# A decoder layer on one core: two small block transfers cut in four, and one PSUM bank of the first phase given to other work

## The chip, the cores and the metric

The kernel runs on one core of a Trainium2 chip. The metric is the device time of one execution in microseconds (us); less is better. Three runs of the kernel before gave 2307.01 to 2318.52 us, with a median of 2308.78 us.

## The reference

One layer of a hybrid decoder is computed for a prompt of 4096 tokens (model width 1024) and for 8 single-token samples. The input is scaled and shifted, projected once, and split into two head groups. Group A is a gated delta rule in chunks, group B an attention with a window of 128. Both are gated, projected back and normalised. The change lies in group A of the prompt:

```python
lower = eye + beta[..., :, None] * jnp.einsum('nbhtd,nbhid->nbhti', k, k) * dec_strict
rhs = jnp.concatenate([(beta * jnp.exp(G))[..., None] * k, beta[..., None] * v], -1)
sol = lax.linalg.triangular_solve(lower, rhs, left_side=True, lower=True, unit_diagonal=True)
...
def step(s, xs):
    w_c, ut_c, aqk_c, qd_c, kd_c, gl_c = xs
    u = ut_c - jnp.einsum('bhcd,bhde->bhce', w_c, s)
    o = jnp.einsum('bhcd,bhde->bhce', qd_c, s) + jnp.einsum('bhti,bhie->bhte', aqk_c, u)
    s = gl_c[..., None, None] * s + jnp.einsum('bhcd,bhce->bhde', kd_c, u)
    return s, o
```

## The kernel before, in words

The work has three phases. The first, which the change touches, makes group A of the prompt in 16 steps of 256 tokens; beside it run the preparation of later weights and the samples' part of group A. The second makes group B in 32 tiles of 128 tokens, and the third the gates, the output projection and the normalisation.

A step of phase one treats two chunks of 128 tokens and four heads, so eight 128 by 128 triangular systems. `front` projects the keys, queries and values (PSUM tile `pj`, lines 300 to 322, with the short convolution on VectorE, L315), takes the decays (tile `pga`, L348), transposes the keys, queries and values (tile `tr`, L355, L389, L399), and multiplies keys by keys and queries (tile `pga`, read by L379 into `U` and by L382 into `Aqk`, four tiles in a step).

`lanes` inverts the 32 by 32 diagonal blocks of the eight systems. It stores them from `U` to a scratch array in HBM in four DMAs (L411), loads them back as `LU`, each block repeated in four groups of 32 partitions (L413), and runs a loop of 31 pairs of VectorE instructions (L420 and L422). The loop works on `LV`, which is first reset from a constant (L415). It stores the result (L424) and loads it back in another order in four DMAs (L429) as `VTd`. Then `gdn_inv` doubles the block size twice (L432 to L480, for each chunk a chain that goes from TensorE to ScalarE, to VectorE and back several times), and `gdn_c` steps the state (L491 to L519).

Side work takes small PSUM tiles from `xt_ps`: the gate's columns (L174, 8 tiles), the samples (`dec_a`, 27 tiles; two for each sample, read by L666 and L678), and the second half of the weights' preparation (`prep_s`, 8 tiles, read by L550). That is 43 tiles in the phase.

PSUM has eight banks here: one for `pga`, one for `xt`, one for `tr`, two for `pj`, three for `pgi` (`gdn_inv` and `gdn_c`). A tile that takes a bank again waits until the last reader of the bank's former tile is done.

The order of the instructions on each engine is set when the program is built. A scheduler goes through all of them with its own estimates of durations, pools and buffers, so that the steps overlap: the loop of one step runs while the next step's projections are made. Each engine then takes its list in that order, and an instruction that waits holds up what is behind it in its own list. All DMAs of the phase's steps are issued by SyncE (SP), in its list's order.

Of the kernel before, what the change touches and what calls it, by code (L numbers as in the profile page):

```python
# [14 lines left out]
PSUM = bass.MemoryType.PSUM  # L15
# [18 lines left out]
def body(ctx, tc, I, O, seq):  # L34
# [3 lines left out]
    pe, act, dve, pool, sp = nc.tensor, nc.scalar, nc.vector, nc.gpsimd, nc.sync  # L38
# [72 lines left out]
    with ExitStack() as p1:  # L111
# [4 lines left out]
        stg = p1.enter_context(tc.tile_pool(name="stg", bufs=2))  # L116
        wk = p1.enter_context(tc.tile_pool(name="wk", bufs=2))
        sml = p1.enter_context(tc.tile_pool(name="sml", bufs=2))
        pga = p1.enter_context(tc.tile_pool(name="pga", bufs=1, space=PSUM))
        pxt = p1.enter_context(tc.tile_pool(name="pxt", bufs=1, space=PSUM))  # L120
        pst = p1.enter_context(tc.tile_pool(name="pst", bufs=1, space=PSUM))
        pj = p1.enter_context(tc.tile_pool(name="pj", bufs=2, space=PSUM))
        pgi = p1.enter_context(tc.tile_pool(name="pgi", bufs=3, space=PSUM))
# [2 lines left out]
            return pst.tile(shape, dt, name="tr")  # L126

        def xt_ps(shape, dt=F32):
            return pxt.tile(shape, dt, name="xt")

        def load_x(s):

# [31 lines left out]
        def gate_cols():  # L164
            part, dst, one = 2, gateT, 1.0
            for blk in range(8):
                cc = part * 8 + blk
                ps = xt_ps([128, 9])
                for hf in range(2):
                    st = stg.tile([128, 4, 256], F32, name="stg")[:, 0:2].rearrange("p a (b c) -> p (a b) c", c=128)  # L170
                    sp.dma_start(st, I["wg"][blk][:, 4 * hf:4 * hf + 4])
                    for k in range(4):
                        mm(ps, st[:, k, :], cT[:, 4 * hf + k, :], hf + k == 0, hf + k == 4)
                dve.tensor_scalar(dst[:, blk, :], ps, cols[:, cc:cc + 1], one, op0=ALU.add, op1=ALU.add)  # L174
                yield
# [84 lines left out]
        def front(s, hT, ahead):  # L260
# [109 lines left out]
            for c in range(2):  # L370
                cs = slice(c * 128, (c + 1) * 128)
                for hp in range(2):
# [8 lines left out]
                    m = 4 * c + 2 * hp  # L381
                    dve.tensor_mul(Aqk[:, m:m + 2, :], pa[:, :, 0, :], decs[c][:, 2 * hp:2 * hp + 2, :])  # L382
            vt, vt16 = lanes(s, U)
            act.activation(U16[:, 0], U, AF.Copy)
            dve.tensor_sub(U16[:, 1], U, U16[:, 0])
# [19 lines left out]
        def lanes(s, U):  # L405

            d1, d2 = D1[s % 2], D2[s % 2]
            d1v = d1.rearrange("(m b) (i t) -> b i m t", b=4, t=32)
            for b in range(4):
                bs = slice(32 * b, 32 * b + 32)  # L410
                sp.dma_start(d1v[b], U[bs, :, bs])  # L411
            LU = w1p.tile([128, 32, 32], F32, name="LU", bufs=1)
            sp.dma_start(LU.rearrange("p a b -> p (a b)"), d1[None].to_broadcast([4, 32, 1024]))  # L413
            LV = w1p.tile([128, 8, 32], F32, name="LV", bufs=1)
            dve.tensor_copy(LV.rearrange("p a b -> p (a b)"), lv0)  # L415
            lt = w1p.tile([128, 8, 32], F32, name="lt", bufs=1)
            for j in range(31, 0, -1):
                j0 = j // 4
                n = 8 - j0
                dve.tensor_mul(lt[:, j0:, 0:j], LV[:, j0:, j:j + 1].to_broadcast([128, n, j]),  # L420
                               LU[:, None, 0:j, j].to_broadcast([128, n, j]))
                dve.tensor_add(LV[:, j0:, 0:j], LV[:, j0:, 0:j], lt[:, j0:, 0:j])  # L422
            d2w = d2.rearrange("l (j c i) -> c l j i", c=4, i=32)
            sp.dma_start(d2w, LV)  # L424
            d2r = d2.rearrange("(m b) (q i) -> b q m i", b=4, i=32)
            vt = VTd
            for b in range(4):
                bs = slice(32 * b, 32 * b + 32)
                sp.dma_start(vt[bs, :, bs], d2r[b])  # L429
            vt16 = w1p.tile([128, 2, 8, 2, 32], F16, name="vt16")  # L430
            ve = vt.rearrange("p m (a b) -> p m a b", b=64)[:, :, :, 0:32]
            act.activation(vt16[:, 0], ve, AF.Copy)  # L432
            dve.tensor_sub(vt16[:, 1], ve, vt16[:, 0])
            return vt, vt16
# [98 lines left out]
        def prep_s(i):  # L533
# [7 lines left out]
            if blk == 0:  # L541
                act.activation(b, b, AF.Copy, scale=WS)
            else:
                gp = xt_ps([128, 2, 2, 128])
                for h in range(2):
                    mm(gp[:, h], gateT[:, 4 * h + u, 0:1].to_broadcast([128, 128]),
                       ident[:, None, :].to_broadcast([128, 2, 128]))
                for row in range(2):
                    q = b[:, 2 * row:2 * row + 2].rearrange("p a b -> p (a b)")
                    dve.scalar_tensor_tensor(q, q, WS, gp.rearrange("p a b c -> p (a b c)"),  # L550
                                             op0=ALU.mult, op1=ALU.mult)
                act.activation(b[:, 0:2], b[:, 0:2], AF.Copy, scale=normc)
# [21 lines left out]
        def dec_a():  # L574
            dt_ = wf
            us_ps = xt_ps([128, 12, 16])
            for blk in range(12):
                w = w1[blk]
# [159 lines left out]
    with ExitStack() as p2:  # L738
# [14 lines left out]
        pst = p2.enter_context(tc.tile_pool(name="pst2", bufs=2, side="right", space=PSUM, **W2))  # L753
# [701 lines left out]
```

## Time and profile before

| what | value |
|---|---|
| median of three runs | 2308.78 us |
| the profiled execution, its own time | 2309.84 us |
| its span, first to last instruction | 2308.1 us |
| TensorE matmul busy | 2119.3 us, 92% |
| VectorE busy | 1834.1 us, 79% |
| ScalarE busy | 1266.6 us, 55% |
| GpSimd busy | 162.0 us, 7% |
| granted TensorE clock, mean | 0.969 |
| share of the last-ending chain: TensorE, VectorE, DMA, ScalarE | 42%, 17%, 7%, 6% |

Busy times overlap between engines. A busy matmul row is not a matmul at its peak, since matmuls are pipelined and their ends are modelled. The chain is followed back from the last instruction: at each step to what released it, or to the instruction ahead of it on its engine. Line numbers are those of the kernel before.

### The profile page before, as it was taken

What the parts mean: (1) busy time and instruction counts of PE and PEld (TensorE: products, weight loads), DVE (VectorE), ACT (ScalarE), POOL (GpSimd) and SP (SyncE); (2) the same over time, 40 slices, a digit from 0 to 9 for tenths busy, and PEclk for the clock granted to TensorE, in tenths of its full rate; (3) what the DMA queues carried; (4) which work ended last, traced back from release to release, by engine and by line L of the source; (5) the groups of instructions that cost most, each with busy time, mean ns of one, the idle gap of its engine ahead of it and who ended that gap; (6) DMA issues with size and microseconds to landing.
All of it is one profiled execution on the core that took longest, in us unless ns stands there. A gap on an engine that the chain in (4) does not pass through costs nothing.

```text
span 2308.1 us, 48753 instructions
## 1 busy us (share of the span) xinstructions
PE 2119.3 (92%) x18287; PEld 1516.0 (66%) x18287; DVE 1834.1 (79%) x5546; ACT 1266.6 (55%) x3601; POOL 162.0 (7%) x284
## 2 busy tenths in 40 slices
PE   6988798898989898899899999999999999999997
PEld 4867677787877787787576777777545454444443
DVE  7778677888888788888767977777687788898877
ACT  6755656666666576666455666666632333434332
POOL 1111110111111011110000000000000000000000
PEclk9999999999999999999899999999999999999999
DMA  8332322323333123222334311111342343333322
GB/s 321 117 114 67 88 88 72 101 89 94 124 101 98 60 76 99 77 67 79 97 102 165 113 59 63 58 59 39 125 169 74 115 141 105 115 106 111 108 91 74
DMA packets 139757, 232.18 MB, mean 101 GB/s; under 512 B 60933, under 2 KB 73529, under 8 KB 133353
## 3 DMA queue, kind: packets, MB, share of 16 engines
q1 hardware_dynamic: 138224, 228.52, 29.5%
q8 instruction: 144, 2.36, 0.4%
q14 instruction: 93, 0.75, 0.1%
q10 hardware_dynamic: 1296, 0.55, 0.1%
HBM read 154.07 MB, written 76.09 MB: 100 GB/s over the span
## 4 chain that ended last, share of the span: by engine, by line
PE 42%; DVE 17%; DMA 7%; ACT 6%; issue 2%; SPq 1%; POOL 0%; POOLq 0%; ACTq 0%; DVEq 0%
PE pp L1040 21%; PE pj L41 9%; DMA LU<-D 3%; PE pgi L41 3%; DVE kqv L315 2%; ACT Sm L870 2%; PE po L41 2%; DVE lt L420 2%; PE tr L887 2%; DVE LV L422 1%; PE tr L41 1%; PE pS L41 1%; DMA D<-LV 1%; DVE bst L1075 1%; PE pga L41 1%
## 5 line engine op out<-in xcount | busy, mean ns | idle before, releaser
L41 PE MATMUL pj<-hT,w 128*128 128x256 f16 x4608 | 578.8, 276 | 3.4 <-ACT hT L255 2.6
L41 PEld LDWEIGHTS <-w 128*128 128x128 f16 x4800 | 452.8, 99 | 62.2 <-issue 6.8
L1040 PEld LDWEIGHTS <-S 128*128 128x128 f16 x1536 | 150.4, 99 | 170.7 <-issue 3.6
L41 PEld LDWEIGHTS <-hT 128*128 128x128 f16 x2048 | 159.8, 98 | 69.3 <-issue 2.0
L41 PE MATMUL pj<-wq,hT 128*128 128x512 f16 x768 | 191.8, 379 | 0.0
L315 DVE SCALAR_TENSOR_TENSOR kqv<-u,cols,kqv 128x256 f32<-128x256 f32 x384 | 181.4, 478 | 2.7 <-ACT kqv L313 2.1
L1040 PE MATMUL pp<-wz,S 128*128 128x512 f16 x768 | 181.1, 382 | 0.0
L870 ACT ACTIVATE Sm<-Sm,nm 128x256 f32<-128x256 f32 (+1 forms) x256 | 125.5, 492 | 92.4 <-DVE nm L867 92.3
L1040 PE MATMUL pp<-wo,S 128*128 128x512 f16 x768 | 171.3, 379 | 0.7 <-DVE zs L1216 0.6
L420 DVE TENSOR_TENSOR lt<-LV,LU 128x60 f32<-128x60 f32 (+24 forms) x496 | 119.4, 241 | 54.9 <-DMA LU<-D 48.8
L1040 PE MATMUL pp<-wz,hT 128*128 128x512 f16 x576 | 133.0, 382 | 1.2 <-ACT zs L1127 1.2
L863 DVE CUSTOM_DVE_ANT_0 Sm<-pS,swam 128x256 f32<-128x256 f32 (+1 forms) x256 | 96.4, 415 | 35.5 <-PE tr L887 32.0
L1040 PE MATMUL pp<-wo,A 128*128 128x512 f16 x540 | 122.1, 379 | 0.0
L41 PE MATMUL pj<-wkv,hT 128*128 128x256 f16 x768 | 107.7, 275 | 0.4 <-ACT v L814 0.4
L1040 PEld LDWEIGHTS <-hT 128*128 128x128 f16 x612 | 60.1, 99 | 72.7 <-issue 4.4
L422 DVE TENSOR_TENSOR LV<-LV,lt 128x60 f32<-128x60 f32 (+24 forms) x496 | 102.6, 207 | 6.2
L41 PE MATMUL pga<-kqv 128*128 128x256 f32 x256 | 75.3, 409 | 25.7 <-DVE kqv L322 25.7
L1079 POOL TENSOR_TENSOR rs<-rs,cf 128x1 f32<-128x1 f32 (+1 forms) x33 | 22.8, 692 | 1077.1 <-DVE rs L1078 1077.1
L1040 PEld LDWEIGHTS <-A 128*128 128x128 f16 x540 | 52.9, 99 | 62.0
L1021 ACT ACTIVATE S<-zt 128x512 f16<-128x512 f32 x64 | 40.2, 630 | 85.3 <-DVE zt L1027 81.1
L1134 ACT ACTIVATE zs<-zs 128x512 f32<-128x512 f32 x48 | 30.2, 629 | 100.5 <-DVE zs L1133 100.5
L315 DVE SCALAR_TENSOR_TENSOR vv<-u,cols,vv 128x256 f32<-128x256 f32 x192 | 82.6, 479 | 1.7 <-ACT vv L313 0.9
(378 smaller groups left out, 4607.0 us busy)
## 6 DMA issues: line engine op xcount, KB each, us to landing
hT<-hD SPq DMA_DIRECT2D x32, 1024.0 KB
x<-in_xT_dram SPq DMA_DIRECT2D x32, 512.0 KB
hD<-hT SPq DMA_DIRECT2D x16, 1024.0 KB
x<-in_x_prompt_dram SPq DMA_DIRECT2D x60, 256.0 KB
out_y_prompt_dram<-x SPq DMA_DIRECT2D x60, 256.0 KB
stg<-in_ws_dram SPq DMA_DIRECT2D x16, 512.0 KB
LU<-D SPq DMA_DIRECT2D x16, 512.0 KB
wS<-wt SPq DMA_DIRECT2D x16, 512.0 KB
```

Source lines behind the costliest of these rows:

```text
L41: pe.matmul(out, l, r, start=st, stop=sp_)
L315: dve.scalar_tensor_tensor(d, u[:, b2, j:j + 256], cwj(j, blk), d, op0=ALU.mult, op1=ALU.add)
L420: dve.tensor_mul(lt[:, j0:, 0:j], LV[:, j0:, j:j + 1].to_broadcast([128, n, j]), LU[:, None, 0:j, j].to_broadcast([128, n, j]))
L422: dve.tensor_add(LV[:, j0:, 0:j], LV[:, j0:, 0:j], lt[:, j0:, 0:j])
L863: dve.tensor_tensor_reduce(Sm[:, h, k0:256], pS[:, h2, k0:256], swam[:, k0:256], 0.125, -1e30, op0=ALU.add, op1=ALU.max, accum_out=mx[:, h ...
L870: act.activation(Sm[:, h, k0:256], Sm[:, h, k0:256], AF.Exp, bias=nm[:, h:h + 1], accum_out=sm_[:, h:h + 1])
L887: pe.transpose(pt[:, h2, kb, :], Sm[:, h + h2, kb * 128:(kb + 1) * 128], ident)
L1021: act.activation(q[:, 0], src, AF.Copy)
L1040: pe.matmul(dst.rearrange("p (u c) -> p u c", c=128), A[:, hi, k, :], W[:, k // 2::2, q, wi, k % 2, :], start=new and n == 0, stop=n == 11 ...
L1075: dve.bn_stats(st[0:n, q, :], r[q][0:n])
L1079: pool.tensor_tensor(rs[0:n, 1:2], rs[0:n, 0:1], half_neg[0:n, 0:1], op=ALU.pow)
L1134: act.activation(zs, zs, AF.Silu, scale=IWS)
```

## The change

The load of `LU` and the store of `LV` become four DMAs each, one for each group of 32 partitions. The pool `xt` goes; what took its tiles now takes them from the single bank of `tr`, and `pga` gets two banks.

```diff
-        pga = p1.enter_context(tc.tile_pool(name="pga", bufs=1, space=PSUM))
-        pxt = p1.enter_context(tc.tile_pool(name="pxt", bufs=1, space=PSUM))
+        pga = p1.enter_context(tc.tile_pool(name="pga", bufs=2, space=PSUM))
...
         def xt_ps(shape, dt=F32):
-            return pxt.tile(shape, dt, name="xt")
+            return pst.tile(shape, dt, name="tr")
...
             LU = w1p.tile([128, 32, 32], F32, name="LU", bufs=1)
-            sp.dma_start(LU.rearrange("p a b -> p (a b)"), d1[None].to_broadcast([4, 32, 1024]))
+            for c in range(4):
+                sp.dma_start(LU[32 * c:32 * c + 32].rearrange("p a b -> p (a b)"), d1)
...
             d2w = d2.rearrange("l (j c i) -> c l j i", c=4, i=32)
-            sp.dma_start(d2w, LV)
+            for c in range(4):
+                sp.dma_start(d2w[c], LV[32 * c:32 * c + 32])
```

The scheduler answers with another order over the whole of phase one. The instructions that compute are the same in kind and number; only SP has more, 6 in a step. Three places follow. In the rows of the change, lines between the two edits are one less than before, and lines behind the second are one more.

VectorE in the ninth step, the last rows ahead of the loop's first instruction, which reads `LU`. Before:

```order
L451 TENSOR_TENSOR Vo<-V,Vo 128x256
L451 TENSOR_TENSOR XE<-pgi,XE 128x8x32
L678 SCALAR_TENSOR_TENSOR stg<-xt,dkq,stg 128x128
L322 SCALAR_TENSOR_TENSOR vv<-th,vv 128x1024
L466 COPY V<-pgi 32x4x32
L467 COPY V<-pgi 32x4x32
L678 SCALAR_TENSOR_TENSOR stg<-xt,dkq,stg 128x128
L256 TENSOR_TENSOR hT<-x,hT 128x512
L451 TENSOR_TENSOR VR<-V,VR 64x256
L256 TENSOR_TENSOR hT<-x,hT 128x512
L451 TENSOR_TENSOR V_319<-pgi,V_319 64x256
L420 TENSOR_TENSOR lt<-LV,LU 128x31
```

And with the change:

```order
L321 SCALAR_TENSOR_TENSOR vv<-th,vv 128x1024
L452 TENSOR_TENSOR XZ<-pgi,XZ 64x4x64
L255 TENSOR_TENSOR hT<-x,hT 128x512 x3
L452 TENSOR_TENSOR Vo<-V,Vo 128x256
L452 TENSOR_TENSOR XE<-pgi,XE 128x8x32
L467 COPY V<-pgi 32x4x32
L468 COPY V<-pgi 32x4x32
L452 TENSOR_TENSOR VR<-V,VR 64x256
L452 TENSOR_TENSOR V_316<-pgi,V_316 64x256
L667 TENSOR_TENSOR dt_9690<-tr,deg 128x4
L420 TENSOR_TENSOR lt<-LV,LU 128x31
```

From the last instruction that fills `U` to that first read of `LU` there were 24 instructions, and there are 27. The second chunk's chain of `gdn_inv` (`Vo` to `V`) stood between other work and now stands in one piece.

VectorE again, from the loop's end of the step ahead to the reset of `LV`, with the change (`vv` and `kqv` are projections, `sc` and `sse` are small vectors):

```order
L422 TENSOR_TENSOR LV<-LV,lt 128x8
L314 SCALAR_TENSOR_TENSOR kqv<-u,cols,kqv 128x256
L321 SCALAR_TENSOR_TENSOR kqv<-th,kqv 128x1024
L359 TENSOR_SCALAR sse<-sse 128x8
...
L314 SCALAR_TENSOR_TENSOR vv<-u,cols,vv 128x256 x6
L378 SCALAR_TENSOR_TENSOR U<-pga,sc,dec 128x128 x2
L381 TENSOR_TENSOR Aqk<-pga,dec 128x256
L378 SCALAR_TENSOR_TENSOR U<-pga,sc,dec 128x128 x2
L381 TENSOR_TENSOR Aqk<-pga,dec 128x256
L415 COPY LV<-cf 128x256
```

All work on the way from the loop's end to the reset is shown but four instructions on small vectors. Behind the reset come four more on `U` and one on `Aqk` before the first that needs `VTd` (L434).

TensorE, in one step, where the weights' preparation takes its product of the gate and the next step's small projection `wbd` begins. Before, in two banks:

```order
L41 MATMUL pgi<-VR,XZ 128x64
L41 MATMUL pgi<-S,kqv 128x128 x4
L41 MATMUL pgi<-r,V 128x128 x4
L41 MATMUL xt<-cf,gateT 128x256
L41 LDWEIGHTS hT
L41 MATMUL tr<-wbd,hT 128x16
```

With the change, in one bank; 29 matmuls lie between the product of the gate and the first on `wbd`:

```order
L41 MATMUL pgi<-S,kqv 128x128 x5
L41 MATMUL tr<-cf,gateT 128x256 x2
L41 LDWEIGHTS w_7_363
L41 MATMUL pj<-hT,w_7_363 128x256
...
L41 MATMUL pgi<-ut,Kd 128x128 x4
L41 MATMUL pgi<-ut,Aqk 128x128 x4
L41 LDWEIGHTS hT
L41 MATMUL tr<-wbd,hT 128x16
```

The side products stood at any place among the transposes. Now, in this step, the three of them (two of a sample, one of the gate) stand behind the step's last transposes, each with 23 to 27 other matmuls ahead of it.

## Rows read from the trace of the kernel before

**Rows 1.** Busy time by stretch: phase one behind its start-up, and phases two, three.
```profile
core 0: us, PE busy (x) PEld busy (x) DVE busy (x) ACT busy (x) POOL busy (x), PEclk, DMA share, GB/s
...
62.00:1155.00 1093.00, 965.24 (x9435) 829.87 (x9432) 891.47 (x3092) 684.92 (x2197) 127.71 (x232) 0.95 0.29 90
...
1200.00:1655.00 455.00, 439.10 (x4853) 315.44 (x4852) 341.46 (x1279) 281.89 (x850) 1.12 (x1) 0.98 0.22 80
1655.00:2308.00 653.00, 627.51 (x3292) 308.13 (x3290) 523.84 (x988) 234.68 (x407) 22.83 (x33) 0.99 0.34 117
```

**Rows 2.** The last-ending chain inside 62 to 1155 us, shares by line.
```profile
by line: DMA LU<-D 6.8%; DVE kqv L315 5.2%; PE pgi L41 4.2%; DVE lt L420 3.6%; PE pj L41 3.1%; DVE LV L422 3.0%; DMA D<-LV 2.2%; issue 2.1%; PE pga L41 1.9%; DMA D<-U 1.4%; DVE wt L557 1.3%; DVE kqv L322 1.0%; SPq L411 0.7%; DVE S L508 0.7%
```

**Rows 3.** Waits of VectorE inside 62 to 1155 us: total us, times, longest.
```profile
DVE lt L420 <- DMA LU<-D: 48.8, 14, 7.3
DVE U L379 <- PE pga L41: 18.4, 15, 2.6
DVE Vo L451 <- ACT Vo L450: 14.0, 12, 2.5
...
DVE LV L415 <- DMA D<-LV: 11.4, 5, 3.2
...
DVE XE L451 <- ACT XE L450: 5.6, 8, 1.2
...
DVE VR L451 <- ACT VR L450: 3.7, 9, 0.6
DVE V L451 <- ACT V L450: 3.5, 9, 0.7
```

**Rows 4.** Waits of TensorE in the same stretch: total us, times, longest.
```profile
PE pgi L41 <- DVE r L491: 15.2, 4, 8.6
PE pgi L41 <- DVE XZ L451: 6.1, 2, 3.2
...
PE xt L41 <- DVE stg L678: 2.7, 1, 2.7
...
PE tr L355 <- ACT Kd L359: 2.8, 12, 0.3
```

**Rows 5.** DMA issues of SP in one step (timeline): start, duration, count.
```profile
699.76 0.56 SPq L424 DMA_DIRECT2D D<-LV  x1
704.57 1.81 SPq L429 DMA_DIRECT2D VTd<-D  x4
713.46 1.78 SPq L411 DMA_DIRECT2D D<-U  x4
716.58 0.54 SPq L413 DMA_DIRECT2D LU<-D  x1
```

**Rows 6.** The same transfers on the chain in order of time: start, duration.
```profile
650.65 10.25 DMA LU<-D
...
699.76 4.74 DMA D<-LV
705.93 1.88 DMA VTd<-D
...
714.79 1.65 DMA D<-U
716.58 8.83 DMA LU<-D
```

**Rows 7.** Busy time by stretch: the start-up, and two flights of the LU load.
```profile
0.00:62.00 62.00, 43.77 (x286) 27.85 (x287) 46.27 (x82) 41.46 (x58) 7.29 (x16) 0.92 0.86 319
...
994.10:1002.40 8.30, 7.78 (x84) 6.69 (x83) 6.90 (x17) 6.36 (x13) 0.19 (x1) 1.00 0.20 65
1059.90:1067.70 7.80, 7.46 (x83) 6.19 (x81) 5.76 (x13) 6.34 (x17) 0.00 (x0) 1.00 0.20 67
```

**Rows 8.** VectorE instructions by form inside 62 to 1155 us: busy us, mean ns.
```profile
L315 DVE SCALAR_TENSOR_TENSOR vv<-u,cols,vv 128x256 f32<-128x256 f32 x192 | 82.6, 479 | 1.7 <-ACT vv L313 0.9
L256 DVE TENSOR_TENSOR hT<-x,hT 128x512 f16<-128x512 f32 x59 | 40.0, 683 | 3.5 <-ACT hT L255 3.4
L379 DVE SCALAR_TENSOR_TENSOR U<-pga,sc,dec 128x128 f32<-128x128 f32 x128 | 39.0, 345 | 19.1 <-PE pga L41 18.4
...
L322 DVE SCALAR_TENSOR_TENSOR vv<-th,vv 128x1024 f32<-128x1024 f32 x16 | 19.5, 1222 | 1.0 <-ACT th L321 0.8
...
L451 DVE TENSOR_TENSOR XE<-pgi,XE 128x256 f16<-128x256 f32 x30 | 12.6, 422 | 6.1 <-ACT XE L450 5.6
```

## The prediction

> **What bounds the kernel now.** I read first how much each engine works in each phase. The change touches phase one alone: 1093 us behind the start-up, 47% of the span [rows 1]. TensorE is busy for 965.2 us of it (88%) and VectorE for 891.5 us (82%); in phases two and three TensorE is at 96%. So phase one has 128 us in which TensorE does nothing, and neither engine is the bound by itself: they wait for each other in the order that was set at the build. A step is a 16th of the phase, 68 us.
>
> Next I looked at what ends last there. On the chain inside the phase the largest single line is a transfer, the load of LU, with 6.8% of 1093 us, or 74 us; the store of LV has 2.2%, or 24 us [rows 2]. The waits of VectorE say the same from the other side: 48.8 us for LU in 14 of the 16 steps, 3.5 us each, and 11.4 us in 5 steps for the store of LV, which must have read LV before it is reset [rows 3]. TensorE in turn waits for what VectorE makes late: 15.2 us for r, 6.1 us for XZ [rows 4]. These stand behind the first read of LU on VectorE, so they are the LU wait, handed on.
>
> Why is the load slow? It takes 8.83 us from issue to landing in one step and 10.25 us in the one ahead, 9.5 us in the mean; four stores of a quarter of 128 KB that go just ahead of it land 1.65 us after the last issue [rows 6]. While it flies alone the 16 DMA engines are busy to 0.20 of their time, at 65 to 67 GB/s; in the start-up, with loads over all 128 partitions, it is 0.86 and 319 GB/s [rows 7]. A share that stays just below a quarter is what four busy engines of 16 make. The load's source has a leading dimension of four repeats, and the store of LV has four groups ahead in its target; the stores and loads of 32 partitions beside them do not.
>
> **The change part by part.**
>
> **The load in four.** Each piece has 32 partitions and 128 KB. SP needs 0.54 us for an issue [rows 5], so the last goes out 3 x 0.54 = 1.6 us behind the first. At 319 GB/s a piece takes 0.41 us, less than the gap between issues, and lands as the small stores do, in 1.65 us: 1.6 + 1.65 + 0.4 = 3.7 us in place of 9.5. The other end, a load no faster than now, would land 1.6 us later than now. I take 3.7, since the rows of 32 partitions are the nearest in shape. From the last write of U the whole way is then 1.78 us of issues [rows 5], 1.65 us of landing and 3.7 us: 7.1 us.
>
> What covers it is VectorE's work between the last U and the first read of LU. In the new order that holds six instructions on vv (2.87 us), one of 1.22 us, four on hT (2.73 us) and nine of the kind of XE (3.80 us), by the durations of [rows 8] 10.6 us without the small ones. So LU is there when it is asked for and the 48.8 us go. If that cover went, the old wait of 3.5 us a step would be back, less the 5.8 us by which LU comes earlier: still nothing.
>
> Something else is late in its place. The second chunk's chain of gdn_inv now stands in one piece ahead of that read, with no other work between its links, and each link goes to TensorE and ScalarE and back. Such links cost VectorE 14.0 + 5.6 + 3.7 + 3.5 = 26.8 us in the phase now, for two chunks in each of 15 steps, 0.9 us a chunk [rows 3]; that is with filling work. Without, I take half as much again and more, 1.5 us: 0.6 us in 16 steps, 10 us back. The ends are 0 (the links are as now) and 48.8 us (they eat all). Term: 48.8 - 10 = 39 us. The chain gives a like figure: 74 us times (9.5 - 3.7)/9.5 is 45 us, and 35 us with the 10 taken off.
>
> **The store in four.** It takes 4.74 us now [rows 6]; in pieces 3 x 0.56 + 1.86, by the neighbouring loads of the same shape [rows 5, 6], or 3.5 us. In the new order 2 instructions on kqv, 6 on vv and 4 on U stand between the loop's end and LV's reset: 0.48 + 1.22 + 2.87 + 1.38 = 5.9 us [rows 8]. The wait of 11.4 us goes; the ends are 0 and 11.4, and I take 11. VTd, which follows with 1.81 us of issues and 1.88 us, is there 7.2 us after the loop. Its first reader on VectorE stands behind 7.3 us of this work and more on Aqk, so that nothing is gained or lost there.
>
> **Issues.** Six more on SP, 3.3 us a step. Behind the load stand the store of hT and the loads of x for the step after next; these have a step's time. Nothing.
>
> **Two banks for the products.** VectorE waits 18.4 us in 15 steps for products in pga [rows 3], of which each step's first is waited for in any case and three come after the bank is read. The ends are 0 and 18.4; I take a third, 6 us, since most of a wait before the first product is for TensorE's place in the order.
>
> **One bank for transposes and side work.** 43 side tiles now take their turn behind others. The nearest price at the low end is the wait of a transpose for the bank's former reader, 2.8 us in 12 cases, 0.23 us [rows 4]; 43 x 0.25 is 11 us lost. The high end is what one side tile waited for its reader on VectorE, 2.7 us [rows 4]: 116 us. I take the low one: between a side tile and the next there are 23 to 29 other matmuls in the new order.
>
> **Sum.** -39 - 11 - 6 + 11 = -45 us on the profiled execution's 2309.8 us, which is 1 us above the median: **2265 us**. TensorE would be busy 965 of 1048 us, 92%, below what it holds in the later phases, so its work does not stop this. [...]
>
> [...]
>
> **The rivals.**
>
> **The split gains nothing in speed.** If the pieces move no faster, LU lands after 1.78 + 1.65 + 1.6 + 9.5 = 14.5 us and the store takes 4.74 + 1.7 = 6.4 us. The cover of LU is 10.6 us and some 2.7 us of small work and links, so that 1.2 us are waited for in 14 steps, 17 us: **2282 us**. For it: nothing of this form is in the trace. Against it: the share of 0.20. This is also the case in which the transfers do not do what the change says.
>
> **A wait in place of the wait.** VectorE reaches LU later because of the chain in one piece, and TensorE's other waits stay. Then only what hangs directly behind LU on TensorE goes: 15.2 + 6.1 + 2.7 = 24 us [rows 4], less 11 for the bank: **2297 us**. For it: 88% is high, and other waits are made of many small ones. Against it: the chain carries 74 us of LU.
>
> **The shared bank becomes the path.** TensorE takes its list in order. If a side tile's readers on VectorE stand late in the loop, the next transpose waits at the head of TensorE's list with all projections behind it. At 2.7 us for each of 43 tiles this is 116 us in place of 11: 2265 + 105 = **2370 us**, slower. It decides from (45 + 11)/43 = 1.3 us a tile. Against it: the order keeps over 20 matmuls between.
>
> **How the numbers follow.** Forecast 0.70, its own range 2240 to 2290; no speed from the split 0.08; a wait in place of the wait 0.13; shared bank 0.09. The measurement can tell about 0.5%, 11.5 us, from no change. Faster takes the forecast, the first rival and half of the second: 0.84. Same takes the other half and a mild case of the third: 0.09. Slower is the rest of the third: 0.07. The low end of the range has all upper ends and a free bank: 48.8 + 11.4 + 18.4 = 78.6 us, 2231. The high end, 2298, takes in the first two rivals.
>
> **What would show it.** Right: LU lands in about 4 us, VectorE's wait for it is nearly gone, the store of LV lands in 3.5 us, r and XZ are no longer waited for. A step takes 68.3 - 45/16 = 65.5 us. Wrong: a like sum of waits on the links of gdn_inv; TensorE waits at tr for VectorE's L678 or L550; or a share of 0.20 still stands while LU flies.

## The result and the profile after

The change takes 2249.24 us in the median of 4 runs (2247.24 to 2251.45), against 2309.13 us for 4 runs of the kernel before: a ratio of 0.9733, with an interval of 0.9705 to 0.9761. On the 2309.8 us of the prediction's sum that is a gain of 62 us (55 to 68), where 45 were forecast. The forecast of faster and its range of 2231 to 2298 held; its size was a quarter too small.

Its profiled execution has a span of 2245.1 us, 63 less than before. The page's head, with busy times and the shares of the chain that ended last:

```profile
PE 2100.4 (94%) x18287; PEld 1495.8 (67%) x18287; DVE 1831.2 (82%) x5546; ACT 1267.1 (56%) x3601; POOL 165.8 (7%) x284
...
PE 54%; DVE 26%; ACT 13%; issue 3%; DMA 3%; POOL 0%; POOLq 0%; ACTq 0%; DVEq 0%; SPq 0%
```

DMA had 7% of the chain and has 3%. The stretches of [rows 1] in the kernel after, and two flights of the LU load as in [rows 7] (busy times, granted clock, DMA share, GB/s):

```profile
62.00:1094.00 1032.00, 950.89 (x9498) 816.87 (x9497) 892.18 (x3100) 687.39 (x2212) 132.31 (x231) 0.98 0.30 95
1139.00:1594.00 455.00, 436.29 (x4823) 312.64 (x4822) 338.18 (x1266) 279.98 (x842) 0.00 (x0) 0.98 0.21 77
1594.00:2245.00 651.00, 625.89 (x3262) 306.64 (x3260) 523.36 (x987) 234.19 (x406) 22.83 (x33) 0.99 0.33 117
610.00:613.00 3.00, 2.77 (x33) 1.99 (x32) 2.92 (x5) 1.92 (x4) 0.37 (x1) 1.00 0.56 175
736.00:739.00 3.00, 2.94 (x26) 2.25 (x24) 2.90 (x7) 2.34 (x4) 0.52 (x1) 1.00 0.59 179
```

Phase one gives 61 us, from 1093 to 1032. It gives them in two ways. TensorE's idle time falls from 1093 - 965.2 = 127.8 us to 1032 - 950.9 = 81.1 us, 47 us less. The same matmuls are also busy for 14 us less, at a granted clock of 0.98 in place of 0.95. While LU flies the DMA engines are now busy to 0.56 and 0.59, at 175 and 179 GB/s, where they had been at 0.20 and 65 to 67 [rows 7].

SP's issues in one step, as in [rows 5]:

```profile
659.35 2.52 SPq L425 DMA_DIRECT2D D<-LV  x4
663.29 1.82 SPq L430 DMA_DIRECT2D VTd<-D  x4
668.60 2.90 SPq L410 DMA_DIRECT2D D<-U  x4
672.84 1.71 SPq L413 DMA_DIRECT2D LU<-D  x4
```

From the first issue of the store of LV to the first of the loads that read it are now 3.9 us (663.29 - 659.35); they were 4.8 [rows 5].

Waits of VectorE inside 62 to 1094 us (total, times, longest), as in [rows 3]:

```profile
DVE gateT L173 <- PE tr L41: 16.4, 8, 4.5
DVE Vo L452 <- ACT Vo L451: 11.8, 10, 2.1
...
DVE VR L452 <- ACT VR L451: 8.6, 12, 1.2
...
DVE U L378 <- PE pga L41: 4.4, 14, 0.5
...
DVE V L452 <- ACT V L451: 2.9, 9, 0.5
...
DVE XE L452 <- ACT XE L451: 1.4, 1, 1.4
...
DVE LV L415 <- DMA D<-LV: 0.5, 1, 0.5
```

No wait for LU is left, and 0.5 us for the store of LV. The links of gdn_inv (Vo, XE, VR, V) take 11.8 + 1.4 + 8.6 + 2.9 = 24.7 us, where they took 26.8 [rows 3]. New is the gate's column: its wait for TensorE is 16.4 us in 8 cases, and before it was

```profile
DVE gateT L174 <- PE xt L41: 2.5, 3, 0.9
```

TensorE in the same stretch, as in [rows 4]:

```profile
PE tr L41 <- DVE g L282: 22.6, 14, 2.6
PE tr L354 <- ACT Kd L358: 7.6, 14, 0.6
...
PE pga L41 <- DVE kqv L321: 4.6, 7, 1.1
PE pgi L41 <- DVE r L492: 4.6, 8, 1.4
```

The wait for r went from 15.2 to 4.6 us, and that for XZ on VectorE is gone. The wait ahead of pga's products was 25.7 us before, 16 times; what ends it is `kqv` (L322), which these products read, and not a reader of the bank's former tile. A transpose's wait for Kd was 2.8 us [rows 4]. No wait of TensorE at `tr` for VectorE's L679 or L551 (the prediction's L678 and L550) is among the rows.

**Where the 14 us of busy time come from.** Three stretches of four microseconds behind one LU load of the kernel before (the load that begins at 716.58 us [rows 6]), in the columns of [rows 1]:

```profile
717.00:721.00 4.00, 3.82 (x55) 3.31 (x51) 3.97 (x13) 4.00 (x9) 0.19 (x1) 1.00 0.21 56
721.00:725.00 4.00, 2.26 (x19) 1.59 (x16) 1.58 (x6) 2.17 (x7) 0.00 (x0) 1.00 0.22 79
725.00:729.00 4.00, 3.05 (x21) 2.62 (x22) 3.04 (x10) 1.24 (x2) 0.00 (x0) 0.63 0.40 116
```

LU lands at 716.58 + 8.83 = 725.4 us. From 721 to 725 us VectorE works for 1.58 us and TensorE for 2.26: both are held while LU is under way. Right behind it TensorE's granted clock is 0.63 in the mean of the stretch, and 0.50 from 726.5 to 729.0 us. Not every LU wait is followed by such a fall. In the step ahead LU lands at 650.65 + 10.25 = 660.9 us, and the clock stays at 1.00:

```profile
657.00:661.00 4.00, 2.73 (x31) 2.19 (x30) 0.65 (x3) 2.69 (x6) 0.00 (x0) 1.00 0.68 196
661.00:665.00 4.00, 2.06 (x43) 2.05 (x44) 3.91 (x10) 1.95 (x5) 0.00 (x0) 1.00 0.26 82
```

Over longer stretches, the third and the fourth 16th of the phase before:

```profile
198.60:266.90 68.30, 55.93 (x528) 47.57 (x526) 49.55 (x166) 41.78 (x135) 7.32 (x13) 0.90 0.29 71
266.90:335.20 68.30, 59.01 (x569) 50.42 (x567) 49.05 (x167) 40.66 (x135) 7.58 (x14) 0.95 0.23 68
```

And with the change:

```profile
191.00:255.50 64.50, 60.83 (x607) 53.05 (x606) 56.06 (x193) 42.02 (x138) 8.75 (x16) 1.00 0.27 85
255.50:320.00 64.50, 60.16 (x610) 51.74 (x609) 56.51 (x190) 52.47 (x158) 11.85 (x16) 1.00 0.35 116
```

The granted clock is 1.00 in both. In the first two 16ths the change is no better: 0.92 and 0.87, against 0.98 and 0.88 before. How the clock goes with the LU wait is shown best by two runs in one order, e4 and e8 below: 0.95 in phase one with 45.4 us of that wait, 0.97 with 1.8 us. A step takes 1032/16 = 64.5 us; 65.5 were forecast.

### The profile page after: what moved, and what is told of

It is laid out like the page before. It is cut to its first block, busy times and chain, and to the rows that moved or that the text cites. A ratio compares the mean times of both kernels' runs of the same rounds, so it can differ in the third digit from the quotient of the medians.

```text
span 2245.1 us, 48856 instructions
## 1 busy us (share of the span) xinstructions
PE 2100.4 (94%) x18287; PEld 1495.8 (67%) x18287; DVE 1831.2 (82%) x5546; ACT 1267.1 (56%) x3601; POOL 165.8 (7%) x284
## 4 chain that ended last, share of the span: by engine, by line
PE 54%; DVE 26%; ACT 13%; issue 3%; DMA 3%; POOL 0%; POOLq 0%; ACTq 0%; DVEq 0%; SPq 0%
PE pp L1041 21%; PE pj L41 12%; PE pgi L41 6%; DVE kqv L314 4%; PE tr L41 3%; PE pga L41 3%; ACT Sm L871 2%; PE po L41 2%; DVE lt L420 2%; PE tr L888 2%; DVE LV L422 2%; DVE vv L314 2%; PE pS L41 1%; DVE wt L558 1%; ACT dec L347 1%
## 5 line engine op out<-in xcount | busy, mean ns | idle before, releaser
L41 PEld LDWEIGHTS <-w 128*128 128x128 f16 x4800 | 447.5, 98 | 65.3 <-issue 14.2
L308 ACT ACTIVATE u<-pj 128x512 f32<-128x512 f32 x96 | 58.9, 613 | 54.2 <-PE pj L41 42.5
```

The costliest lines, as they stand in the source:

```text
L41: pe.matmul(out, l, r, start=st, stop=sp_)
L308: act.activation(u[:, :, 3:259], ps, AF.Copy, scale=IWS)
```

## The experiments

Ratios are to the kernel before, from runs on the same chip; 1% is 23.1 us. Edits are against the kernel before unless it is said that they are against the change.

### The parts alone

**Both splits, banks as before (e1_split_only).**

```diff
-            sp.dma_start(LU.rearrange("p a b -> p (a b)"), d1[None].to_broadcast([4, 32, 1024]))
+            for c in range(4):
+                sp.dma_start(LU[32 * c:32 * c + 32].rearrange("p a b -> p (a b)"), d1)
...
-            sp.dma_start(d2w, LV)
+            for c in range(4):
+                sp.dma_start(d2w[c], LV[32 * c:32 * c + 32])
```

> Both transfers in four DMAs, PSUM banks as before. Theory 1 (the transfers make the gain): the waits of VectorE for LU (48.8 us) and for the store of LV (11.4 us) go, 45 to 60 us are won, 2250 to 2265 us. Theory 2 (the banks and the order that comes with them make it): 2295 to 2310 us, and other waits stand where the LU wait was.

Measured: 0.9673 (0.9642 to 0.9703), 2238.8 us. The splits alone give 76 us, more than the whole change and more than either theory had. Its chain in one step (start, duration) holds an LU load of four pieces, from the first issue to the last landing:

```profile
739.71 0.32 SPq L414
...
741.01 2.68 DMA LU<-D
```

From the first issue to landing are 741.01 + 2.68 - 739.71 = 4.0 us, where 3.7 had been worked out. VectorE's longest wait is now another one, from 62 to 1088 us:

```profile
DVE U L379 <- PE pga L41: 35.9, 34, 3.1
```

It was 18.4 us [rows 3]. In e4, where LU is still waited for, it is 32.3 us, so it is another order that makes it longer, and not the LU wait's going.

**The banks alone (e2_banks_only).**

```diff
-        pga = p1.enter_context(tc.tile_pool(name="pga", bufs=1, space=PSUM))
-        pxt = p1.enter_context(tc.tile_pool(name="pxt", bufs=1, space=PSUM))
+        pga = p1.enter_context(tc.tile_pool(name="pga", bufs=2, space=PSUM))
...
-            return pxt.tile(shape, dt, name="xt")
+            return pst.tile(shape, dt, name="tr")
```

> New PSUM banks, both transfers as one DMA each. Theory 1: LU lands 9 to 10 us after its issue as before, VectorE waits for it 30 to 50 us in all, time 2295 to 2315 us. Theory 2: 2250 to 2270 us.

Measured: 1.0019 (1.0000 to 1.0039), 2318.8 us. Two of VectorE's waits in it:

```profile
DVE lt L419 <- DMA LU<-D: 49.5, 15, 5.8
DVE LV L414 <- DMA D<-LV: 29.8, 11, 5.1
```

The LU wait stays, the wait for the store of LV grows from 11.4 us, and the banks alone gain nothing. The time is 4 us above the range of Theory 1.

**The LU split alone (e3_lu_only)**, the first hunk of e1.

> The load of LU in four DMAs alone; the store of LV whole and the banks as before. Theory 1: the 48.8 us for LU go and the 11.4 us for the store stay: 2262 to 2275 us. Theory 2: 2295 to 2310 us. If the store matters as much as the load, over 2285 us.

Measured: 0.9691 (0.9666 to 0.9716), 2241.5 us, or 71 us gained. This one edit is nearly all of e1, and it is 20 us below the range that Theory 1 gave it. Phase one:

```profile
62.00:1089.00 1027.00, 944.09 (x9471) 812.53 (x9469) 887.35 (x3075) 689.64 (x2218) 128.52 (x234) 0.99 0.31 95
```

VectorE has no wait for LU in it. Its wait for the store of LV, which is still one DMA here, has gone from 11.4 us [rows 3] to

```profile
DVE LV L416 <- DMA D<-LV: 4.2, 4, 1.8
```

so the new order alone takes most of what the LV split was to bring. Idle time of TensorE falls by 127.8 - 82.9 = 45 us and its busy time by 965.2 - 944.1 = 21 us.

**The LV split alone (e4_lv_only)**, the second hunk of e1.

> The store of LV in four DMAs alone, LU whole, banks as before. If the store counts for little: 2300 to 2312 us, VectorE's wait for LU stays at 45 us or more. If it counts by itself: below 2295 us.

Measured: 0.9932 (0.9906 to 0.9958), 2294.9 us: 16 us, with 10 to 22 in the interval. So the store counts by itself, and the LU wait stays at 45.4 us all the same. On top of the LU split it gives nothing that can be told from zero (e1 against e3).

### A faster load, or a longer way to its reader?

In e3 there are 26 to 41 VectorE instructions between the last `U` from `pga` and the first read of `LU`, from the third step on, against 17 to 27 before: the scheduler answered to four DMAs by putting more work ahead. (That it rates four dearer than one is inferred from its orders.) So the edit changes two things, how fast LU lands and how late it is asked for. Three runs part them.

**Four slow pieces in e3's order (e7_slow_pieces).** The scratch array gets four groups of rows with a gap, so that each piece has a leading dimension of four. All operations of VectorE, ScalarE and TensorE stand in exactly e3's order.

```diff
-    D1 = [dr.tile([32, 1024], F32, name=f"D1_{i}") for i in range(2)]
+    D1 = [dr.tile([4, 9, 1024], F32, name=f"D1_{i}") for i in range(2)]
...
-            d1v = d1.rearrange("(m b) (i t) -> b i m t", b=4, t=32)
+            d1v = d1[:, 0:8].rearrange("b m (i t) -> b i m t", t=32)
...
-            sp.dma_start(LU.rearrange("p a b -> p (a b)"), d1[None].to_broadcast([4, 32, 1024]))
+            for c in range(4):
+                sp.dma_start(LU[32 * c:32 * c + 32].rearrange("p a b -> p (a b)"), d1[:, 0:8])
...
-            d2r = d2.rearrange("(m b) (q i) -> b q m i", b=4, i=32)
+            d2r = d2.rearrange("(b m) (q i) -> b q m i", b=4, i=32)
```

> The same order of all engines as with the load of LU alone in four DMAs of 32 partitions, but the source's rows stand in four groups with a gap, so that each piece has a leading dimension of four: slow pieces in the new order. Theory a (speed): LU flies at a share near 0.2 for 9 to 11 us, VectorE waits for it 20 to 50 us, 2280 to 2310 us. Theory b (order): the longer way to the first read hides the slow load, wait under 10 us, 2238 to 2255 us.

Measured: 0.9663 (0.9635 to 0.9690), 2234.2 us, no slower than e3 and 4 us under Theory b's range. One flight:

```profile
611.70:620.50 8.80, 8.31 (x93) 6.93 (x92) 8.50 (x21) 7.76 (x20) 0.60 (x1) 1.00 0.17 61
```

The pieces are as slow as the old load (0.17 and 61 GB/s for 8.8 us), and VectorE still never waits for LU: it is busy for 8.50 of these 8.8 us. With e3's order, speed is worth nothing.

**One fast load in e4's order (e8_lane_major).** The load stays one DMA, with the repeat behind the rows, and the store and the constant follow the new order of the lanes. All operations stand in exactly e4's order, so this pair shows what the speed alone does.

```diff
-            sp.dma_start(LU.rearrange("p a b -> p (a b)"), d1[None].to_broadcast([4, 32, 1024]))
+            sp.dma_start(LU.rearrange("p a b -> p (a b)"), d1[:, None].to_broadcast([32, 4, 1024]))
...
-            sp.dma_start(d2w, LV)
+            for c in range(4):
+                sp.dma_start(d2w[c], LV[c:128:4])
...
-            lane[p, jj, 4 * jj + p // 32] = 1.0
+            lane[p, jj, 4 * jj + p % 4] = 1.0
```

> The same order of all engines as with the store in four DMAs alone, but the repeat of four of the LU load stands behind the 32 rows and not ahead of them: one DMA, same bytes, leading dimension 32. Theory a (the speed of the load on the chip makes the gain): the load flies at a share of 0.5 or more and lands in 3 to 4 us, VectorE's wait for it is under 5 us, 2240 to 2265 us. Theory b (the new order makes the gain, since the scheduler counts four DMAs as dearer and puts more work ahead of the first read): 2290 to 2312 us.

Measured: 0.9687 (0.9658 to 0.9716), 2239.6 us, at the low edge of Theory a's range. Two flights, and the LU wait at the first read (a row of the page's costliest groups; behind the bar busy time, mean ns, and idle time ahead with its releaser):

```profile
611.20:613.70 2.50, 2.29 (x30) 1.86 (x28) 2.29 (x8) 2.50 (x6) 0.20 (x1) 1.00 0.61 198
675.40:677.90 2.50, 2.42 (x31) 2.29 (x32) 2.36 (x10) 2.44 (x5) 0.20 (x1) 1.00 0.64 205
```

```profile
L420 DVE TENSOR_TENSOR lt<-LV,LU 128x60 f32<-128x60 f32 (+24 forms) x496 | 119.0, 240 | 8.0 <-DMA LU<-D 1.8
```

In this order speed is worth 0.9932 - 0.9687 = 0.0245, or 57 us. Phase one of e4 and then of e8, each up to the same instruction, the end of the last loop:

```profile
62.00:1145.00 1083.00, 966.83 (x9410) 833.43 (x9409) 890.41 (x3090) 686.79 (x2197) 124.28 (x232) 0.95 0.29 90
62.00:1081.00 1019.00, 943.54 (x9396) 813.57 (x9394) 886.96 (x3083) 682.38 (x2193) 125.04 (x231) 0.97 0.30 95
```

TensorE is idle for 116.2 us in e4 and for 75.5 in e8, 41 less, and busy for 23 less, at a granted clock of 0.97 in place of 0.95. The order is the same, and of the transfers only LU's differs in speed as far as the waits tell (the store's pieces take every fourth partition, and the wait for them is 0.3 us in e4 and 0.4 in e8), so both come from the load. How VectorE's wait gets to TensorE can be read in TensorE's own waits, of e4:

```profile
PE pgi L41 <- DVE V L452: 17.1, 7, 4.6
...
PE pgi L41 <- DVE XZ L452: 12.9, 3, 6.0
```

In e8 they are 0.2 and 1.3 us. What stands behind the first read of LU on VectorE hands the wait on, as the prediction read it. So either a faster load or the other order, with its longer way to the reader, gives nearly the whole gain, and the two don't add:

| | short way (e4's order) | longer way (e3's order) |
|---|---|---|
| slow load | 0.9932 (e4) | 0.9663 (e7) |
| fast load | 0.9687 (e8) | 0.9691 (e3) |

The left column has the LV split too, the right one has not, and the two orders differ over all of phase one. So the speed alone is compared only within a column; that the right column gains by the longer way, and by nothing else in its order, is likely but not shown.

**Four pieces by columns (e5_lu_columns)**, against the change: each piece keeps the leading repeat of four and all 128 partitions.

```diff
-            for c in range(4):
-                sp.dma_start(LU[32 * c:32 * c + 32].rearrange("p a b -> p (a b)"), d1)
+            for q in range(4):
+                sp.dma_start(LU[:, 8 * q:8 * q + 8].rearrange("p a b -> p (a b)"), d1[None, :, 256 * q:256 * q + 256].to_broadcast([4, 32, 256]))
```

> As the change, but the four DMAs of the LU load are cut by columns: each has all 128 partitions and 128 KB, with the repeat of four as its leading dimension. Same bytes, same number of DMAs. If the leading dimension sets how many DMA engines work: LU flies for 9 to 11 us at a DMA share near 0.2 as before, and some of the wait for it is back, 2255 to 2300 us. If the number of DMAs sets it: 4 us, a share of 0.5 or more, and 2249 us as with the change.

Measured: 0.9862 (0.9836 to 0.9889), 2281.9 us, inside the range for a leading dimension that decides, with an LU wait back. The wait, and of its chain in one step the first issue and the last landing:

```profile
DVE lt L420 <- DMA LU<-D: 30.5, 14, 3.7
```

```profile
624.91 0.57 SPq L413
...
626.69 7.47 DMA LU<-D
```

From the first issue to landing are 626.69 + 7.47 - 624.91 = 9.25 us, as long as the one load took before, though there are four DMAs. (Other loads flew beside LU, so its own share can't be read cleanly.) Its order has 17 to 24 instructions ahead of the read, and 1.3% on the change is lost, 30 us. Since the order differs from the change's, this isn't the price of speed alone.

**What this leaves open for the change itself.** No run has slow pieces in the change's own order. In the step whose issues of LU begin at 672.84 us, shown above, the first read is

```profile
682.26 0.21 DVE L420 TENSOR_TENSOR lt<-LV,LU 128x31 f32<-128x31 f32 x1
```

9.4 us behind the first issue, and from the third to the fifteenth step it is 9.4 to 12.2 us, and VectorE does not wait right ahead of it. Slow pieces land 8.4 to 10.9 us behind the first issue, by e5's waits. So it is an estimate from these two that slow pieces would have been waited for little in the change too, and how its gain divides between the speed and the new order stays open.

### The banks, with both splits

| run | banks of pga | banks of tr | side work in | ratio |
|---|---|---|---|---|
| e1_split_only | 1 | 1 | a bank of its own | 0.9673 |
| e9_shared_one_pga | 1 | 1 | tr | 0.9879 |
| the change | 2 | 1 | tr | 0.9733 |
| e10_tr2 | 1 | 2 | tr | 0.9797 |
| e6_gate_pga | 2 | 1 | tr, but the gate's in pga | 0.9693 |
| e12_side_in_pgi | 2 | 1 | pgi | 0.9792 |
| e11_side_in_pga | 2 | 1 | pga | 0.9621 |

**Sharing alone (e9_shared_one_pga)**, against the change; seven banks are in use.

```diff
-        pga = p1.enter_context(tc.tile_pool(name="pga", bufs=2, space=PSUM))
+        pga = p1.enter_context(tc.tile_pool(name="pga", bufs=1, space=PSUM))
```

> Both splits, side work in the transposes' bank, the products with one bank again (one of the eight banks unused). If the sharing costs 10 us or more and the products' second bank gives some of it back: 2255 to 2275 us, and VectorE waits 30 us or more for the products again. If the second bank gives nothing: 2245 to 2255 us, as the change.

Measured: 0.9879 (0.9845 to 0.9913), 2291.4 us, 16 us above the dearer of the two ranges. VectorE's waits from 62 to 1140 us:

```profile
DVE gateT L173 <- PE tr L41: 22.0, 8, 5.9
DVE U L378 <- PE pga L41: 20.4, 19, 1.6
DVE VR L452 <- ACT VR L451: 12.8, 16, 2.4
...
DVE XZ L452 <- ACT XZ L451: 10.0, 7, 2.5
```

Sharing tr costs 0.9879 - 0.9673 = 0.0206, 48 us. The second bank of pga then gives 0.9879 - 0.9733 = 0.0146, 34 us, back. The gate's columns wait longest, 22.0 us against 2.7 in e1; the links VR and XZ wait 12.8 and 10.0 us against 5.1 and 4.9. The wait for U is 20.4 us, not the 30 or more that was expected. Of TensorE's waits at `tr` only one row, 0.3 us, is ended by a side tile's reader on VectorE (the gate's column). The row that grew there is a product's wait for `g`, which it reads, 21.8 us against 11.8. So transposes that wait behind side tiles are not what the rows show; the larger part of the price stands in VectorE's waits.

The wait for U tells pga's banks apart in every run: 18.4 to 35.9 us with one bank (before, e1, e3, e4, e7, e8, e9, e10), 4.2 to 7.2 with two (the change, e2, e5, e6, e11, e12).

**Two banks for the shared pool (e10_tr2)**, against the change:

```diff
-        pga = p1.enter_context(tc.tile_pool(name="pga", bufs=2, space=PSUM))
-        pst = p1.enter_context(tc.tile_pool(name="pst", bufs=1, space=PSUM))
+        pga = p1.enter_context(tc.tile_pool(name="pga", bufs=1, space=PSUM))
+        pst = p1.enter_context(tc.tile_pool(name="pst", bufs=2, space=PSUM))
```

> Both splits; transposes and side work share a pool of two banks, the products keep one. Theory 1 (the shared single bank costs the change some 10 us against the split alone, the products' second bank brings nothing): 2230 to 2243 us, at or under the split alone. If the products' second bank brings something that the sharing eats: 2243 us or more.

Measured: 0.9797 (0.9763 to 0.9831), 2265.7 us. That is the second case. The freed bank is worth 0.0082 (19 us) here, against 34 us as pga's second.

**The gate's tiles in pga (e6_gate_pga)**, against the change:

```diff
-                ps = xt_ps([128, 9])
+                ps = pga.tile([128, 9], F32, name="pga")
```

> As the change, but the eight gate tiles alone (16.4 us of VectorE's waits) take the products' banks. If these waits carry the change's loss against the split alone: 2232 to 2243 us. If they are one wait among others: 2243 to 2250 us.

Measured: 0.9693 (0.9664 to 0.9722), 2248.2 us. Its interval overlaps that of the change, so the eight gate tiles alone are not shown to matter, as the second case said.

**All side work in pga (e11_side_in_pga)**, against the change:

```diff
         def xt_ps(shape, dt=F32):
-            return pst.tile(shape, dt, name="tr")
+            return pga.tile(shape, dt, name="pga")
```

> Both splits, two banks for the products, and the side work in these two and not in the transposes' bank. If it is the transposes' bank that the side work costs the change: 2225 to 2240 us, VectorE waits for the gate's columns under 8 us. If side work costs wherever it shares: 2245 us or more.

Measured: 0.9621 (0.9594 to 0.9647), 2230.1 us. It is faster than both kernels, and than the change by 0.9733 - 0.9621 = 0.0112, or 26 us. So the transposes' bank is a dearer host than the two of pga. Against the splits alone (e1) the intervals overlap, so no use of the banks here is shown to gain on e1. Phase one, and VectorE's waits for the two kinds of tiles in it (for the gate's columns under 8 us were expected):

```profile
62.00:1080.00 1018.00, 941.25 (x9432) 815.30 (x9430) 890.03 (x3086) 681.93 (x2198) 130.09 (x232) 0.98 0.31 96
```

```profile
DVE gateT L173 <- PE pga L41: 12.6, 8, 2.0
...
DVE U L378 <- PE pga L41: 7.2, 16, 1.7
```

**All side work in pgi (e12_side_in_pgi)**, as e11 with `pgi` in place of `pga`.

> As the change, but the side work takes the three banks of the inversion and the state's step (pgi), not the transposes' one. If only the transposes' single bank is a bad host: 2225 to 2243 us. If a pool in which tiles are already handed on in a long chain is a bad host too: 2245 us or more, with more waits of VectorE and TensorE on pgi than with the change.

Measured: 0.9792 (0.9764 to 0.9820), 2269.4 us. Sharing the three banks of gdn_inv is worse than sharing tr, though the gate's columns wait only 6.4 us there: VectorE's waits for products in `pgi` add up to 31 us against 18 with the change, and TensorE's waits ahead of its work there to 36 against 30, as was expected of a pool with a long chain.

## Why the prediction was right, and where it was off

**What bounds phase one** was read rightly. The LU load was the largest line of the chain [rows 2], and the LU split alone gives 71 us.

**The load in four.** The flight is 4.0 us for 3.7, the share rises from 0.20 to over 0.55, and the 48.8 us of waits [rows 3] go. What was off is the size: the term of 39 us measured 71 (66 to 77) in e3. Two parts of it were wrong. The "10 us back" for the chain in one piece did not come; the links take 24.7 us, not 26.8 plus 10. And TensorE's clock, 0.95 in phase one [rows 1] and 0.99 in e3, had no part in the sum: of e3's gain TensorE's busy time makes 21 us and its idle time 45, and the second is near the 48.8 us of the wait. In one order, e4 against e8, it is 23 and 41 us. The line of the chain, 74 us [rows 2], came nearer here than the wait on one engine; that is one case. Taking 5.8/9.5 of it cut too much: no LU wait was left, so all of it went.

The mechanism was half told. The prediction put the gain down to speed and named the cover as something that only had to be there. In e4's order the speed is what gains (e8); in the order that the scheduler made of four DMAs alone, the cover would have done without it (e7). The cover itself, 10.6 us and some 2.7 of small work, was worked out well: from the last U to the first read of LU the change takes 13.5 to 18.8 us from the third step on.

**The store in four.** Forecast 11, measured 16 (10 to 22) by itself: right. Its loads follow its first issue by 3.9 us, where 3.5 were worked out for the flight. Beside the LU split it can't be told from nothing, since e3's order takes the wait from 11.4 to 4.2 us by itself; the terms overlap and should not have been added in full.

**Two banks for the products** was forecast at 6 us with 18.4 as the upper end, and measured 34, beyond it. The end was VectorE's wait for U in the kernel before, and that wait is not a fixed one: it is 35.9 us in the order of both splits (e1). Nor is only a third of it the bank's: with the second bank it falls from 20.4 (e9) to 4.4 us, four fifths. The rest of the 34 us is spread over other waits, the gate's columns (22.0 to 16.4) and the links VR and XZ among them; no run takes it apart. TensorE's wait ahead of pga for kqv, 25.7 us before and 4.6 now, does not follow the banks: it is 24.2 us in e1 and 11.4 in e9 with one bank, and 24.3 in e11 with two.

**One bank for transposes and side work** was forecast at 11 us and measured 48, inside its ends of 11 and 116, at 1.1 us a tile. The low end was taken for the 23 to 29 matmuls between two side tiles; that was no protection. Both ends were priced by TensorE's waits at a bank, and the rows of e9 hardly show such waits: the larger part stands in what VectorE waits for, the gate's columns above all. Together the two terms were forecast at 5 us lost and came to 14 lost (e1 against the change, with intervals that touch almost: 0.9703 and 0.9705). Two errors of 37 and 28 us nearly cancelled, which is luck, and the undersized LU term decided the total: -71 of LU, little more for LV, +14 for the banks.

**The rivals.** "The split gains nothing in speed" fell as stated: the share is not 0.20 but 0.56 and 0.59. Its time of 2282 us need not have followed either, since e7 has the old speed in pieces and loses nothing; only e5, with a shorter way, comes near it (2281.9). "A wait in place of the wait" did not come on the links; another wait grew, that for U, by 17.5 us in e1, and the gain came all the same. "The shared bank becomes the path" came near in price, 1.1 us a tile in e9 where 1.3 was its point of decision, but its mechanism, transposes held at the head of TensorE's list by a side tile's reader, is hardly in TensorE's waits, with 0.3 us in e9; the second bank of pga took most of the price back.

In these runs it is the leading dimension that made the load slow, not the count of DMAs: four DMAs with a leading dimension of four are slow in e7 (0.17 and 61 GB/s over 8.8 us) and e5 (9.25 us from the first issue to landing), and one DMA over 128 partitions with its repeat behind the rows is fast in e8 (0.61 and 0.64). That four of the 16 engines were busy is the prediction's estimate from the share of 0.20; no run shows how many were.

**What stays open.** Each bank variant has another order throughout phase one. The runs show what each costs, not which of its instructions makes e10 and e12 worse than e11. That the four slow pieces of e7 cost nothing is shown for this order alone; for the change's own order it is an estimate.

## What to carry to other kernels

When a transfer's wait is taken off a path that holds several engines, look at its line on the chain beside the wait on one engine (here 74 and 48.8 us, for a measured 71), and look whether the granted clock drops behind the wait: what comes back there can be a gain of its own (23 us from e4 to e8). Before crediting an edit of a DMA with speed, hold the order fixed and change the speed, and the reverse; a scheduler that sees four DMAs in place of one may have moved the reader. When an edit changes the order, read all the waits again: that for U doubled from 18.4 to 35.9 us in e1. Sharing a PSUM bank had a price here (48 us for tr), and which pool took the guests (2230 to 2269 us for three choices) mattered as much as the second bank did (34 us).

## What the runs showed of the hardware

One 512 KB load moved at 65 to 67 GB/s with its repeat of four ahead of the rows [rows 7] and at 198 to 205 GB/s with the repeat behind them (e8), for the same bytes and partitions. Four pieces whose source has a leading dimension of four moved at 61 GB/s together in one flight (e7). Behind one stretch in which TensorE worked for 2.26 of 4 us, its granted clock was 0.63 in the mean of the next; behind another, with 2.73 of 4 us, it stayed at 1.00. With the change the two stretches from 191 to 320 us that are shown above have 1.00.
